# Order of the f32 matmuls in sample attention: strip by strip, or piece by piece over four strips

## Chip, core and metric

The kernel runs on one core of a Trainium2 chip. The metric is the device time of one execution in microseconds; of several runs the median is taken. The engines are named as the profile names them: PE is TensorE (PEld its weight loads), DVE is VectorE, ACT is ScalarE, POOL is GpSimd, and SP issues most of the loads.

## The reference, cut to what matters

The kernel computes one layer of a decoder for 1024 prompt positions and for 8 samples of 4 new positions each, with a cache of 1024 earlier positions for each sample. Only the attention of the samples is touched by the change. Each sample's 4 positions attend, in 12 query heads (3 dilations times 4 key/value heads of 64 dimensions), to 129 positions of cache and new rows that lie 1, 4 or 16 apart:

```
def dilated_attn_sample(q, k_all, v_all, L):
    ...
    for g, (_, dil) in enumerate(DIL_PAIRS):
        idx = L + jnp.arange(T)[:, None] - dil * taps[None, :]
        ...
        s = jnp.einsum('bthd,btkhd->bthk', q[:, :, g], kg, preferred_element_type=jnp.float32) * (HEAD_DIM ** -0.5)
        s = s - (slopes[g] * dil)[:, None] * taps.astype(jnp.float32)[None, :]
        m = jnp.max(s, axis=-1, keepdims=True)
        p = jnp.exp(s - m)
        outs.append(jnp.einsum('bthk,btkhd->bthd', p, vg) / den[..., None])
    return combine_groups(outs, lses)
```

The slope of a head makes far positions count less, and positions before the first are masked. The kernel gets both as a mask that is added to the scores.

## The kernel before, in words

Activations lie with the features on the 128 partitions and the 1056 positions (1024 of the prompt, 32 of the samples) in the columns. Projections multiply in three terms of split halves (`wh`, `wl`), through the helper at L122, in blocks of 352 columns; a block of a projection (`proj`) is 24 matmuls into one of two PSUM banks named `mm`. The weights stream in by SP, are split by ACT (L115) and DVE (L116), and wait in rings of three.

The stage around the change computes the twelve projections of the convolution branch (L1047 on; four features f of three units each). After each block of a projection `tick()` takes one step of a chain of generators: first the mixing of the prompt's attention groups, then four sample groups (`sample_set`, L665 on), then `sample_sum`. After the third feature (f = 2) whatever is left of the chain is written out at once. Which instruction stands where in the queue of an engine is then settled by the framework, which keeps dependences and orders by its own estimate of when inputs are there; in this stage the order of the code isn't pinned.

A sample group is one pair of key/value heads (hp) and four samples (bg): there are four groups. For each, SP loads a mask and five tiles of 1024 columns, `kv[0]` to `kv[4]`, with the cache's keys and values. The four samples of a group are the four strips: sample j has its query weights in 32 columns (`qs`), and its results on the partitions 32 j to 32 j + 31 of a PSUM bank. The steps of a group are these:

- Scores (L682 to L684): for each sample, one matmul over 512 columns of keys into the bank `pa`, one over 128 columns into `pb`, and one over the 32 new positions (`kS`) into `pb`.
- Softmax: DVE adds the mask and takes the maximum (L688, L692), ACT takes the exponential (L698).
- Transposes on PE (L705, L708, L709), copied to `pT` by DVE (L706, L710, L711).
- Values (L719, L723): for each sample five matmuls of 128 keys each against tiles of `kv[2]` to `kv[4]`, and one of the 32 new positions against `v_smp`, all summed in one place of the bank `po`. L719 has 128 rows and 32 columns of weights, L723 32 and 32.
- ACT copies `po` to `oS` (L727).

Between two steps lies a block of a projection, whose bank is emptied by ACT (L1054) or by DVE (L1062). ACT and DVE work through their queues in order, so what stands behind L727 waits for the values too. After the fourth group come `sample_sum` (L812 to L854) and the last three projections.

The prompt's attention, earlier, has a loop of the same kind with two strips of 64 columns (L580): there the head, which selects the strip, is the inner loop.

Of the kernel before, what the change touches and what calls it, by code (L numbers as in the profile page):

```python
# [14 lines left out]
P = 128  # L15
# [3 lines left out]
TS = 32  # L19
# [39 lines left out]
def tile_decoder_step(ctx: ExitStack, tc: tile.TileContext, i, o):  # L59
    nc = tc.nc  # L60
# [16 lines left out]
    def U(dt=F32, w=T):  # L77
        return up.tile([P, w], dt, tag="U", name=nm("U"))
# [8 lines left out]
    def psum(tag=None):  # L87

        if tag is None:
            turn[0] += 1  # L90
            tag = ("mm", "s", "s")[turn[0] % 3]
        return pp.tile([P, 512], F32, tag=tag, name=nm(tag), bufs=banks[tag])
# [4 lines left out]
    def const(name, shape, src=None, dt=F32):  # L97
        t = cp.tile(shape, dt, tag=name, name=name)
        if src is not None:
            fill(t, src)  # L100
        return t

    def small(shape, tag, bufs=2, dt=F32):
        return sp.tile(shape, dt, tag=tag, name=nm(tag), bufs=bufs)
# [33 lines left out]
    def fill(out, in_):  # L138

        with tc.issue_after(pace[0].ins):  # L140
            nc.sync.dma_start(out=out, in_=in_)
# [35 lines left out]
    def rstd(*sums, out=None, soon=True):  # L177

        w = sums[0].shape[-1]
        n = w // 32  # L180
        ps = norm_bank()
        with tc.high_priority() if soon else nullcontext():
            for q, s in enumerate(sums):
                matmul(ps[:, :w], ones, s, start=q == 0, stop=q == len(sums) - 1)

        t = tmp("tb")[:, :w]
        nc.vector.transpose(t, ps[:, :w])
        r = small([P, 12], "r4")[:, :n]
        tv = t.rearrange("p (c q) -> p c q", q=32)
        nc.scalar.activation(r, tv[:, :, 0], AF.Sqrt, bias=eps_t, scale=1.0 / D)  # L190
        nc.vector.reciprocal(r, r)
        nc.vector.tensor_copy(tv, r.unsqueeze(2).to_broadcast([P, n, 32]))
        if out is None:
            out = small([P, LW], "rstd", 1)[:, :w]
        nc.vector.transpose(out, t)
        return out
# [156 lines left out]
    kS = const("kS", [P, 2, TS])  # L353
# [103 lines left out]
    for n in range(9):  # L457
        r = P if n < 8 else TS
# [35 lines left out]
    qs = const("qs", [P, 2, 8, 32])  # L494
# [36 lines left out]
    for g in range(3):  # L531
# [28 lines left out]
        for hp in range(2):  # L560
# [29 lines left out]
            for n in range(8):  # L590
# [8 lines left out]
                for h in range(2):  # L599
# [6 lines left out]
                        start=True,  # L606
                        stop=True,
# [57 lines left out]
    def sample_set(se):  # L665

        hp, bg = se // 2, se % 2
        msk = U()
        fill(msk[:, :NKS], i["maskS"][se])
        kv = [U() for _ in range(5)]  # L670
        for q in range(5):
            fill(kv[q][:, :1024], i["kv"][hp, bg, q])
        if se == 0:
            fill(hmask, i["hmask"])
        for _ in range(3):
            yield
        pa, pb = psum("s"), psum("s")
        for j in range(4):
            b = bg * 4 + j
            qb = qs[:, hp, b, :]  # L680
            r = slice(32 * j, 32 * j + 32)
            nc.tensor.matmul(pa[r, :512], qb, kv[j // 2][:, (j % 2) * 512 : (j % 2 + 1) * 512], start=True, stop=True)  # L682
            nc.tensor.matmul(pb[r, :P], qb, kv[2][:, j * P : (j + 1) * P], start=True, stop=True)
            nc.tensor.matmul(pb[r, P : P + TS], qb, kS[:, hp, :], start=True, stop=True)  # L684
        s = msk
        m0 = small([P, 1], "m0")
        m = stS[:, 0, se : se + 1]
        nc.vector.tensor_tensor_reduce(  # L688
            out=s[:, :512], in0=pa, in1=msk[:, :512], scale=1.0, scalar=-3.0e38,
            op0=ALU.add, op1=ALU.max, accum_out=m0,  # L690
        )
        nc.vector.tensor_tensor_reduce(  # L692
            out=s[:, 512:NKS], in0=pb[:, :160], in1=msk[:, 512:NKS], scale=1.0, scalar=m0,
            op0=ALU.add, op1=ALU.max, accum_out=m,
        )
        nm_ = small([P, 1], "nms")
        nc.vector.tensor_scalar(out=nm_, in0=m, scalar1=-1.0, scalar2=None, op0=ALU.mult)
        nc.scalar.activation(  # L698
            s[:, :NKS], s[:, :NKS], AF.Exp, bias=nm_, accum_out=stS[:, 1, se : se + 1]
        )  # L700
        yield
        pT = U()
        tp = psum("t")
        for c in range(4):
            nc.tensor.transpose(tp[:, c * P : (c + 1) * P], s[:, c * P : (c + 1) * P], ident)  # L705
        nc.vector.tensor_copy(pT[:, :512], tp)  # L706
        tp = psum("t")
        nc.tensor.transpose(tp[:, :P], s[:, 512:640], ident)  # L708
        nc.tensor.transpose(tp[:TS, P : 2 * P], s[:, 640:NKS], ident)  # L709
        nc.vector.tensor_copy(pT[:, 512:640], tp[:, :P])  # L710
        nc.vector.tensor_copy(pT[:TS, 640:768], tp[:TS, P : 2 * P])  # L711
        yield
        po = psum("o")
        for j in range(4):
            r = slice(32 * j, 32 * j + 32)
            for c in range(5):
                m = j * 5 + c + 4
                vc = kv[2 + m // 8][:, (m % 8) * P : (m % 8 + 1) * P]
                nc.tensor.matmul(  # L719
                    po[r, :P], pT[:, c * P + 32 * j : c * P + 32 * j + 32], vc,  # L720
                    start=c == 0, stop=False,
                )
            nc.tensor.matmul(  # L723
                po[r, :P], pT[:TS, 640 + 32 * j : 640 + 32 * j + 32], v_smp[:, hp * P : (hp + 1) * P],
                start=False, stop=True,
            )
        nc.scalar.copy(oS[:, se, :], po[:, :P])  # L727
        yield
# [131 lines left out]
    def conv(f, z, yb):  # L860
# [29 lines left out]
        yield  # L890

    attn = chain(mix_groups(), *(sample_set(se) for se in range(4)), sample_sum())
    taps = iter(())

# [538 lines left out]
    for b, ts in enumerate(LB):  # L1433
        w = ts.stop - ts.start
        before, sums = sums, [small([P, LW], "ssum", 3)[:, :w]]
        for f in range(KD):
# [9 lines left out]
            if f == 1 and b:  # L1446
                r = rstd(*before, soon=False)
# [171 lines left out]
```

## Time and profile before

| what | value |
|---|---|
| median of 3 runs | 1720.37 us (1718.62 to 1722.14) |
| the profiled execution | 1723.34 us, span 1721.6 us |
| mean granted clock of PE | 0.991 |
| PE busy | 1686.6 us, 98% of the span |
| DVE busy | 1018.8 us, 59% |
| ACT busy | 572.9 us, 33% |

The groups of the changed lines, from the view that groups instructions by line: the columns are line, engine, operation, what it writes and reads, count; then the busy time of the group, the mean length of one in ns, and the engine's idle time before them.

```profile
L719 PE MATMUL o<-U,U 128*32 128x128 f32 x160 | 20.5, 275 | 0.0
L682 PE MATMUL s<-U,qs 128*32 128x512 f32 x32 | 13.2, 605 | 0.0
L723 PE MATMUL o<-v_smp,U 32*32 32x128 f32 x32 | 6.4, 280 | 0.0
L683 PE MATMUL s<-U,qs 128*32 128x128 f32 x32 | 5.0, 276 | 0.0
L684 PE MATMUL s<-kS,qs 128*32 128x32 f32 x32 | 3.0, 194 | 0.0
```

Busy time is the time in which at least one instruction of the group runs, so for instructions that overlap it is less than count times length. A matmul's length runs until its last result is out, and the next one can start before that. The forms are the size of the part of PE that is used (rows * columns of weights) and what streams through it (partitions x columns).

### The profile page before, as it was taken

Reading aid. Unit: us, or ns where it says so; the run is one execution under the profiler, and the core shown is the slowest. Engines: PE = TensorE matmul, PEld = TensorE weight load, DVE = VectorE, ACT = ScalarE, POOL = GpSimd, SP = SyncE. Lnnn points to the kernel's source line nnn. Section 1 sums busy time; section 2 is a strip of 40 time slices with the busy share of each in tenths; the row PEclk is TensorE's granted clock in tenths of the full one; section 3 lists DMA queues with packets and bytes.
Section 4 is the critical chain, followed back from the end, with each engine's and each line's share of the span. In section 5 each row is a group of like instructions: output and inputs, shape, how many; then the busy total and the mean of one; then the engine's idle time right before and its main releaser. Section 6 shows DMA issues by size and latency. Waiting matters only on the chain.

```text
span 1721.6 us, 28876 instructions
## 1 busy us (share of the span) xinstructions
PE 1686.6 (98%) x12041; PEld 1624.8 (94%) x12041; DVE 1018.8 (59%) x1895; ACT 572.9 (33%) x1072; POOL 34.4 (2%) x42
## 2 busy tenths in 40 slices
PE   8999999999999999999999899999999999999996
PEld 7999878888889999999999899999999999999996
DVE  7437454453255544557767886555555554777658
ACT  7321243411123333341256563333332224421021
POOL 0001000000000000000000000000000000000005
PEclk9999999999999999999999999999999999999998
DMA  6332212062522232276453403222222224433202
GB/s 214 129 108 101 88 39 62 18 214 77 192 71 98 103 113 101 102 266 205 157 194 129 157 26 100 78 85 83 92 75 75 75 75 175 175 100 116 84 1 101
DMA packets 74410, 191.69 MB, mean 111 GB/s; under 512 B 11836, under 2 KB 33660, under 8 KB 74280
## 3 DMA queue, kind: packets, MB, share of 16 engines
q1 hardware_dynamic: 48624, 144.23, 25.4%
q10 hardware_dynamic: 25656, 45.63, 7.3%
q8 instruction: 94, 1.54, 0.4%
q14 instruction: 36, 0.29, 0.1%
HBM read 143.16 MB, written 46.67 MB: 110 GB/s over the span
## 4 chain that ended last, share of the span: by engine, by line
PE 91%; DVE 5%; issue 1%; ACT 1%; DMA 0%; DVEq 0%; ACTq 0%
PE pair L122 35%; PE mm L122 19%; PE bank L122 14%; PE s L122 12%; PE s L602 2%; PE t L635 1%; PE o L719 1%; PE o L580 1%; PE s L382 1%; PE s L381 1%; PE s L383 1%; DVE U L1426 1%; PE s L682 1%; DVE ssum L1445 1%; DVE wl L116 1%
## 5 line engine op out<-in xcount | busy, mean ns | idle before, releaser
L122 PE MATMUL pair<-U,wh 128*128 128x264 f32 x2880 | 526.5, 284 | 0.0
L122 PEld LDWEIGHTS pair<-U,wh 128*128 128x128 f32 x2880 | 445.9, 188 | 0.0
L122 PE MATMUL pair<-U,wl 128*128 128x264 f32 x1440 | 408.6, 284 | 0.0
L115 ACT CAST wh<-wr 128x512 fp32r<-128x512 f32 (+1 forms) x262 | 191.3, 742 | 512.8 <-PE pair L122 174.6
L122 PE MATMUL mm<-U,wh 128*128 128x352 f32 (+1 forms) x1280 | 316.9, 327 | 2.3 <-ACT U L1054 2.0
L122 PEld LDWEIGHTS pair<-U,wl 128*128 128x128 f32 x1440 | 271.2, 188 | 0.0
L122 PE MATMUL bank<-U,wh 128*128 128x352 f32 (+2 forms) x1056 | 256.0, 325 | 0.2 <-DVE U L116 0.2
L116 DVE TENSOR_TENSOR wl<-wr,wh 128x512 fp32r<-128x512 f32 (+1 forms) x262 | 216.0, 838 | 63.9 <-ACT wh L115 62.2
L122 PEld LDWEIGHTS mm<-U,wh 128*128 128x128 f32 x1280 | 221.4, 190 | 15.1 <-issue 8.8
L122 PE MATMUL mm<-U,wl 128*128 128x352 f32 (+1 forms) x648 | 208.5, 322 | 0.0
L122 PE MATMUL s<-U,wh 128*128 128x352 f32 (+1 forms) x888 | 198.5, 311 | 6.2 <-ACT U L263 5.8
L122 PEld LDWEIGHTS bank<-U,wh 128*128 128x128 f32 x1056 | 185.9, 189 | 1.0 <-DVE U L116 0.5
L122 PE MATMUL bank<-U,wl 128*128 128x352 f32 (+2 forms) x528 | 171.7, 325 | 0.7 <-DVE wl L116 0.7
L122 PEld LDWEIGHTS s<-U,wh 128*128 128x128 f32 x888 | 149.8, 190 | 8.4 <-ACT U L263 6.2
L122 PE MATMUL s<-U,wl 128*128 128x352 f32 (+1 forms) x468 | 144.1, 308 | 0.0
L1413 DVE TENSOR_TENSOR U<-bank,U 128x352 f32<-128x352 f32 x192 | 97.3, 522 | 51.7 <-PE bank L122 51.7
L122 PEld LDWEIGHTS mm<-U,wl 128*128 128x128 f32 x648 | 122.7, 189 | 1.7 <-issue 1.3
L115 ACT CAST U<-U 128x1056 fp32r<-128x1056 f32 (+2 forms) x111 | 82.0, 757 | 91.5 <-DMA U<-a_dram 31.1
L116 DVE TENSOR_TENSOR U<-U,U 128x1056 fp32r<-128x1056 f32 (+2 forms) x111 | 92.6, 856 | 30.8 <-ACT U L115 30.4
L1009 DVE TENSOR_TENSOR tb<-pair,ta 128x528 f32<-128x528 f32 x49 | 34.7, 708 | 120.4 <-PE pair L122 120.4
L122 PEld LDWEIGHTS bank<-U,wl 128*128 128x128 f32 x528 | 99.9, 189 | 1.4 <-DVE wl L116 1.4
L122 PEld LDWEIGHTS s<-U,wl 128*128 128x128 f32 x468 | 88.8, 190 | 0.0
(282 smaller groups left out, 1887.6 us busy)
## 6 DMA issues: line engine op xcount, KB each, us to landing
wr<-in_w SPq DMA_DIRECT2D x143, 512.0 KB, 4.0
sig_dram<-V ACTq DMA_DIRECT2D x24, 528.0 KB, 2.7
V<-sig_dram SPq DMA_DIRECT2D x24, 528.0 KB, 3.7
a_dram<-U ACTq DMA_DIRECT2D x22, 528.0 KB, 5.0
U<-a_dram SPq DMA_DIRECT2D x22, 528.0 KB, 5.2
U<-in_kv SPq DMA_DIRECT2D x20, 512.0 KB, 6.9
U<-outs SPq DMA_DIRECT2D x10, 528.0 KB, 6.5
U<-in_xT SPq DMA_DIRECT2D x24, 176.0 KB, 4.6
```

Of the source, the lines that this page charges most:

```text
L115: nc.scalar.copy(hi, x)
L116: (eng or nc.vector).tensor_tensor(out=lo, in0=x, in1=hi.bitcast(F32), op=ALU.subtract)
L122: ins = nc.tensor.matmul(*a, **k)
L381: nc.tensor.matmul(ps[:, :HV], h_hi[k][:, tk], wv[k][0], start=k == 0, stop=False)
L382: nc.tensor.matmul(ps[:, :HV], h_hi[k][:, tk], wv[k][1], start=False, stop=False)
L383: nc.tensor.matmul(ps[:, :HV], h_lo[k][:, tk], wv[k][0], start=False, stop=k == KD - 1)
L580: nc.tensor.matmul(po[0][h * 64 : (h + 1) * 64, (n % 4) * P : (n % 4 + 1) * P], vg[kb // 4][:, (kb % 4) * 256 + hd : (kb % 4) * 256 + hd + ...
L602: nc.tensor.matmul(ps, qT[hs_, n * P : (n + 1) * P], kg[hp][hs_, k0 : k0 + nk * P], start=True, stop=True,)
L635: last = nc.tensor.transpose(tp[:, at : at + P], pt[:, h, c * P : (c + 1) * P], ident)
L682: nc.tensor.matmul(pa[r, :512], qb, kv[j // 2][:, (j % 2) * 512 : (j % 2 + 1) * 512], start=True, stop=True)
L1009: nc.vector.tensor_tensor(out=out, in0=view(ps), in1=y, op=ALU.add)
L1413: nc.vector.tensor_tensor(out=a, in0=ps, in1=a, op=ALU.add)
```

## The change

Both loops over strips are turned inside out. In the scores, all four samples' matmuls of 512 columns come first, then all four of 128, then all four of 32. In the values the loop over the five pieces of keys is the outer one and the samples are the inner one, and the four matmuls of the new positions stand behind in a loop of their own. Operands, tiles, counts and flags stay the same, and nothing but these PE instructions is moved in the code.

```
         pa, pb = psum("s"), psum("s")
-        for j in range(4):
-            b = bg * 4 + j
-            qb = qs[:, hp, b, :]
-            r = slice(32 * j, 32 * j + 32)
-            nc.tensor.matmul(pa[r, :512], qb, kv[j // 2][:, (j % 2) * 512 : (j % 2 + 1) * 512], start=True, stop=True)
-            nc.tensor.matmul(pb[r, :P], qb, kv[2][:, j * P : (j + 1) * P], start=True, stop=True)
-            nc.tensor.matmul(pb[r, P : P + TS], qb, kS[:, hp, :], start=True, stop=True)
+        rows = [slice(32 * j, 32 * j + 32) for j in range(4)]
+        qb = [qs[:, hp, bg * 4 + j, :] for j in range(4)]
+        for j, r in enumerate(rows):
+            nc.tensor.matmul(
+                pa[r, :512], qb[j], kv[j // 2][:, (j % 2) * 512 : (j % 2 + 1) * 512], start=True, stop=True
+            )
+        for j, r in enumerate(rows):
+            nc.tensor.matmul(pb[r, :P], qb[j], kv[2][:, j * P : (j + 1) * P], start=True, stop=True)
+        for j, r in enumerate(rows):
+            nc.tensor.matmul(pb[r, P : P + TS], qb[j], kS[:, hp, :], start=True, stop=True)
...
         po = psum("o")
-        for j in range(4):
-            r = slice(32 * j, 32 * j + 32)
-            for c in range(5):
+        for c in range(5):
+            for j, r in enumerate(rows):
                 m = j * 5 + c + 4
                 vc = kv[2 + m // 8][:, (m % 8) * P : (m % 8 + 1) * P]
                 nc.tensor.matmul(
                     po[r, :P], pT[:, c * P + 32 * j : c * P + 32 * j + 32], vc,
                     start=c == 0, stop=False,
                 )
+        for j, r in enumerate(rows):
             nc.tensor.matmul(
                 po[r, :P], pT[:TS, 640 + 32 * j : 640 + 32 * j + 32], v_smp[:, hp * P : (hp + 1) * P],
                 start=False, stop=True,
```

## The prediction

> **What bounds the kernel now.** I read the page first (busy shares, then the chain that ended last).
>
> ```profile
> span 1721.6 us, 28876 instructions
> PE 1686.6 (98%) x12041; PEld 1624.8 (94%) x12041; DVE 1018.8 (59%) x1895; ACT 572.9 (33%) x1072; POOL 34.4 (2%) x42
> ...
> PE 91%; DVE 5%; issue 1%; ACT 1%; DMA 0%; DVEq 0%; ACTq 0%
> ```
>
> TensorE is busy for 98% of the span and is 91% of the chain, so time taken out of its stream comes off the end, as long as nothing else becomes late. The changed lines run in the stretch from 376 to 486 us, so I next asked for the busy time by windows, there and behind it.
>
> ```profile
> 376.00:486.00 110.00, 107.98 (x705) 90.43 (x704) 31.19 (x80) 14.85 (x29) 0.00 (x0) 0.99 0.41 149
> 486.00:530.00 44.00, 44.00 (x263) 43.65 (x263) 31.82 (x39) 16.18 (x21) 0.00 (x0) 0.95 0.27 87
> 530.00:600.00 70.00, 70.00 (x560) 70.00 (x560) 33.06 (x51) 25.03 (x42) 0.00 (x0) 1.00 0.23 88
> ```
>
> The columns are the length, the busy time of TensorE, its weight loads, VectorE, ScalarE and GpSimd, the clock, the DMA share and GB/s. TensorE is busy for 107.98 of the 110 us; VectorE has 31.19 us of work and ScalarE 14.85. Behind it TensorE has no idle time up to 600. So this stage ends when TensorE's stream ends, and the stages behind take over any shift.
>
> Then I asked for windows cut to the changed stages themselves, each from the first matmul of a stage to the start of the next matmul that isn't of it. The last row of each answer adds the stages up: first the scores of groups 1 to 3 (L682 to L684), then the values of all four groups (L719, L723).
>
> ```profile
> sum 11.76, PE 11.76 PEld 5.68 DVE 1.04 ACT 0.90 POOL 0.00; mean PE 3.92 PEld 1.89 DVE 0.35 ACT 0.30 POOL 0.00
> ```
> ```profile
> sum 24.64, PE 24.64 PEld 18.29 DVE 7.13 ACT 0.45 POOL 0.00; mean PE 6.16 PEld 4.57 DVE 1.78 ACT 0.11 POOL 0.00
> ```
>
> Three score stages of 3.92 us and four value stages of 6.16, all of it TensorE alone. The scores of group 4 look different, and they are used below.
>
> **What a strip costs now.** The timeline of the first score stage shows what one strip waits for (start, length, what). Every f32 matmul call is two instructions, which I call passes; the rows count them (x2 for the first strip's one call of L682).
>
> ```profile
> 379.76 1.05 PE L682 MATMUL s<-U,qs 128*32 128x512 f32 x2
> ...
> 380.65 0.62 PE L682 MATMUL s<-U,qs 128*32 128x512 f32 x1
> 380.75 0.27 PE L683 MATMUL s<-U,qs 128*32 128x128 f32 x1
> ...
> 380.86 0.23 PE L684 MATMUL s<-kS,qs 128*32 128x32 f32 x2
> 381.10 0.59 PE L682 MATMUL s<-U,qs 128*32 128x512 f32 x1
> ...
> 381.53 0.27 PE L683 MATMUL s<-U,qs 128*32 128x128 f32 x1
> ```
>
> Inside a strip a pass starts when the one before has been streamed: 381.53 - 381.10 = 0.43 us for 512 columns (0.45 for the first pass of a run, 381.10 - 380.65), 380.86 - 380.75 = 0.11 for 128. For the 32 columns of L684 I estimate a quarter of that, 0.03. The next strip's first pass begins at 380.65, while the first strip still has a pass of L683 (380.75) and both of L684 (380.86) to start. So two strips do run beside each other, and a later matmul in another strip starts ahead of earlier ones. Still, the wide passes of the four strips come one after another: the second strip's start 380.65 - 379.76 = 0.89 us behind the first's.
>
> The values show no overlap at all. Rows of TensorE's own timeline, from a narrow window last:
>
> ```profile
> 392.37 1.28 PE L719 MATMUL o<-U,U 128*32 128x128 f32 x10
> 393.58 0.40 PE L723 MATMUL o<-v_smp,U 32*32 32x128 f32 x2
> 393.91 1.28 PE L719 MATMUL o<-U,U 128*32 128x128 f32 x10
> ```
> ```profile
> 398.00 0.27 PE L719 MATMUL o<-U,U 128*32 128x128 f32 x1
> 398.20 0.40 PE L723 MATMUL o<-v_smp,U 32*32 32x128 f32 x2
> 398.53 0.43 PE L122 MATMUL mm<-U,wh 128*128 128x352 f32 x1
> ```
>
> Each strip is ten passes of tile 128*32, then two of tile 32*32, and the next strip starts only after them: 393.91 - 392.37 = 1.54 us, four times. The step from one tile size to the other takes 398.20 - 398.00 = 0.20 us where a pass of the same tile would follow after 0.11, and the way back out of L723 takes 398.53 - 398.20 = 0.33 for its two passes and the switch.
>
> **What four strips cost side by side.** Group 4 shows it already. Its scores were split up by the framework that orders the instructions: two strips of L682, then projection matmuls, the other two strips, more projection, and all of L683 and L684 together.
>
> ```profile
> 466.28 1.05 PE L682 MATMUL s<-U,qs 128*32 128x512 f32 x4
> 467.26 0.43 PE L122 MATMUL mm<-U,wh 128*128 128x352 f32 x1
> ...
> 470.90 0.45 PE L683 MATMUL s<-U,qs 128*32 128x128 f32 x8
> 471.14 0.26 PE L684 MATMUL s<-kS,qs 128*32 128x32 f32 x8
> 471.34 0.43 PE L122 MATMUL mm<-U,wh 128*128 128x352 f32 x1
> ```
>
> Four passes of 512 columns in two strips take 1.05 us, which is what the two of one strip took at 379.76: the second strip is free. Eight passes of 128 columns in four strips take 0.45 us, where two in one strip take 0.40 (L723 rows): all four run together, and the fourth lags by about 0.04 us. The prompt's attention says the same of two strips for longer, twelve passes of L580 (64 columns each) in 0.88 us, where ten in one strip take 1.28:
>
> ```profile
> 200.87 0.88 PE L580 MATMUL o<-tb,U 128*64 128x128 f32 x12
> ```
>
> **The change, part by part.** It removes and adds no instruction; it puts the four strips of one piece next to each other.
>
> Scores of groups 1 to 3. In each strip the six passes follow one another as now: 0.45 + 0.43 for L682, 0.11 + 0.11 for L683, 0.03 for L684; add 0.04 of lag and 0.13 for the way back to the projection's tile (471.34 less the last start of L684, which I put at 471.14 + 0.03 + 0.04 = 471.21). That is 1.30 us instead of 3.92: 2.62 less, three times, 7.9 us.
>
> Scores of group 4. They stay as they are if the framework splits them as before, so 0. If it doesn't, the three pieces (467.26 - 466.28 = 0.98 twice, 471.34 - 470.90 = 0.44) become one of 1.30, and two entries of about 0.09 go: another 1.3 us. Split like this, groups 1 to 3 would lose the same 1.3 us each, 3.9. I take neither: these bounds go to the range.
>
> Values, four groups. Ten passes of a strip have their starts spread over 1.28 - 0.27 = 1.01 us; with lag 1.05 for four strips at once. Then one switch, 0.20, and L723 with its way out, 0.33 + 0.04. That is 1.62 us instead of 6.16: 4.54 less, four times, 18.2 us. About 0.55 of each 4.54 is the six switches that go (0.09 each); the rest is overlap.
>
> Waits. The fourth strip's first value matmul needs the last of the five loaded tiles, which is asked for now only in the third strip; the matmuls of the next projection are queued behind such a wait. What it costs is bounded by when the tiles land.
>
> ```profile
> L141 SPq DMA_DIRECT2D U<-in_kv x20: 327/404/646, 348.8 to 446.3; - x20
> ...
> DMA to landing us min/median/max: 3.6/6.9/9.4
> ```
>
> The last load is issued at 446.3 and lands by 446.3 + 9.4 = 455.7. The scores of group 4 start at 466.28. Between the issue and the scores lie the shortened scores and values of group 3, 2.6 + 4.5 = 7.1 us, so the scores come 466.28 - 446.3 - 7.1 = 12.9 us behind the last issue, over 9.4; the values come later still. Earlier groups have longer. So I take nothing. The softmax between scores and values (VectorE, ScalarE) is covered by a block of 24 projection matmuls as now, at 0.16 us each (below) 3.9 us. If a wait comes after all, its price is itself and perhaps a clock drop:
>
> ```profile
> 481.54 0.27 ACT L727 COPY V<-o 128x128 f32<-128x128 f32 x1 [8.47 <-PE o L723]
> ...
> 483.84 0.95 PE L122 MATMUL mm<-U,wh 128*128 128x352 f32 x2 [2.02 <-ACT U L1054]
> ```
> ```profile
> 483.80:491.00 7.20, 7.16 (x26) 6.76 (x27) 5.73 (x15) 0.38 (x2) 0.00 (x0) 0.54 0.27 97
> 491.00:530.00 39.00, 39.00 (x244) 38.85 (x244) 27.35 (x32) 16.12 (x21) 0.00 (x0) 1.00 0.30 99
> ```
>
> Behind the last values ScalarE had stood at L727; the copies that empty the projection's banks were queued behind it, and TensorE idled 2.0 us. Then the clock was 0.54 for 7.2 us: 26 matmuls, which at the next row's 39.00/244 = 0.16 us each would take 4.2, so 3.0 us were lost. The order behind the last values is unchanged, so I leave both in; the drop may go (3.0 less) or come once more (3.0 more). The Trainium skill ("TensorE: Matmul & The Clock Gate", Part 1) says that the clock halves after an idle window of about 3.4 us; this trace shows a drop after 2.0 us, so the row sets my bound. By the skill's length neither 3.0 would belong to the range.
>
> Sum: 7.9 + 18.2 = 26.1 us. The profiled execution took 1723.34 us, its span of 1721.6 and 1.7 around it; so 1697.2 for it. It stands 2.97 above the median of the three runs, 1720.37, so I forecast a median of **1694.3 us**.
>
> **Rivals.**
> *Overlap, but only in part.* Either no more than two strips stream at once, or matmuls start strictly in program order, so that a strip's second pass holds up the next strip and each new strip costs one pitch. Two at once: values 1.62 + 1.01 = 2.63 and scores 1.30 + 0.88 + 0.25 = 2.43, a gain of 4 x 3.53 + 3 x 1.5 = 18.6, 1701.8 us. In order: values 20 x 0.11 (a second pass with the next strip's first) + 0.9 for L723 and its switches = 3.1, scores 4 x (0.43 + 0.11 + 0.03) + 0.15 = 2.4, a gain of 4 x 3.06 + 3 x 1.5 = 16.7, 1703.7. For it: 512 columns in four strips, and more than 0.45 us of four strips, are in no row. Against it: the start at 380.65 ahead of 380.75, and the eight passes in 0.45. The second form is what the Trainium skill would have ("TensorE: Matmul & The Clock Gate", Part 3, The mechanism): it says that matmuls start and end strictly in program order; the rows at 380.65 and 470.90 differ from that.
> *TensorE idles behind each shortened stage* (the slower side). ScalarE stands at the copy behind a stage until the stage ends, as at 481.54, and the two banks of the projection aren't emptied in time; each place pays 2.3 us of idle (483.84 - 481.54) and 3.0 of low clock, 5.3. Six shortened stages have no such gap now (groups 1 to 3): 6 x 5.3 = 31.8 - 26.1 = 5.7 us slower, 1726. It decides from five stages on (26.5). For it: the rows at 481.54. Against: at 398.53 the projection follows the values at once, and a shorter stage holds ScalarE for less time.
> *The change doesn't take effect.* The framework orders instructions by its own idea of when inputs arrive, as in group 4, and puts the strips one by one again: 1720. Against: in groups 1 to 3 the trace follows the order of the code.
>
> **How the numbers follow.** The forecast gets 0.90, partial overlap 0.06, idling 0.02, no effect 0.02. Its own range: 1694.3 - 1.3 - 3.0 = 1690.0 to 1694.3 + 3.9 + 3.0 = 1701.2; the runs shown lie up to 1.8 from their median (1718.62 to 1722.14), so 1688 to 1703, which also takes in the first form of partial overlap. About 0.2% (3.4 us) is what a measurement can tell from no change. Faster: 0.90 + 0.06 = 0.96; same 0.02; slower 0.02.
>
> **What would show it.** In the new timeline: L719 as one row of 40 passes of some 1.3 us, followed by one row of eight passes of L723; L682 as eight passes in about 1.1 us; the next projection 1.6 and 1.3 us behind the first matmul. Value stages over 2.5 us mean partial overlap; a projection that names ScalarE or VectorE as what it waited for, with a clock near 0.5 behind it, means idling. Wrong outright: stages as short as said but an end that hasn't moved, with TensorE's idle time grown elsewhere.

## The result, and the profile after

| what | before | after |
|---|---|---|
| median | 1720.02 us (4 runs, 1718.62 to 1722.14) | 1693.64 us (4 runs, 1691.83 to 1695.26) |
| profiled execution, span | 1723.34 us, 1721.6 us | 1693.98 us, 1692.2 us |

The ratio is 0.9846 (95% interval 0.9834 to 0.9858): 26.4 us less in the medians, where 26.1 was forecast. The page of the changed kernel, with the busy shares and the chain that ended last:

```profile
span 1692.2 us, 28872 instructions
PE 1657.3 (98%) x12041; PEld 1604.4 (95%) x12041; DVE 1018.9 (60%) x1895; ACT 573.1 (34%) x1072; POOL 34.5 (2%) x42
...
PE 92%; DVE 4%; issue 1%; ACT 1%; DMA 0%; DVEq 0%; ACTq 0%
```

As many matmuls as before, but TensorE is busy for 29.3 us less (1686.6 to 1657.3), and its share of the span is the same 98%. VectorE and ScalarE do the same work in the shorter span.

The first group in TensorE's timeline after the change; L681, L685 and L687 are the scores (L682 to L684 before), L721 and L726 the values (L719 and L723 before):

```profile
379.08 1.06 PE L681 MATMUL s<-U,qs 128*32 128x512 f32 x8
379.97 0.40 PE L685 MATMUL s<-U,qs 128*32 128x128 f32 x8
380.19 0.24 PE L687 MATMUL s<-kS,qs 128*32 128x32 f32 x8
380.36 0.43 PE L122 MATMUL mm<-U,wh 128*128 128x352 f32 x1
```
```profile
389.03 1.30 PE L721 MATMUL o<-U,U 128*32 128x128 f32 x40
390.26 0.42 PE L726 MATMUL o<-v_smp,U 32*32 32x128 f32 x8
390.61 0.59 PE L122 MATMUL mm<-U,wh 128*128 128x352 f32 x2
```

The counts are what to look at. Forty passes of L721 lie in one row of 1.30 us; before, ten took 1.28. Eight passes of 512 columns take 1.06 us, where the two of a single strip took 1.05. The windows over the stages, cut as before (sum rows; three score stages, four value stages):

```profile
sum 3.82, PE 3.82 PEld 1.90 DVE 0.89 ACT 0.90 POOL 0.00; mean PE 1.27 PEld 0.63 DVE 0.30 ACT 0.30 POOL 0.00
```
```profile
sum 6.32, PE 6.32 PEld 4.73 DVE 2.58 ACT 0.45 POOL 0.00; mean PE 1.58 PEld 1.18 DVE 0.65 ACT 0.11 POOL 0.00
```

11.76 - 3.82 = 7.94 us for the scores (7.9 forecast) and 24.64 - 6.32 = 18.32 for the values (18.2 forecast): 26.26 in all. The scores of group 4 are split into three pieces as before. Behind the last values TensorE idles as before, for the same time:

```profile
456.87 0.59 PE L122 MATMUL mm<-U,wh 128*128 128x352 f32 x2 [2.02 <-ACT U L1057]
```

The two profiled executions differ by more than the stages, 29.4 us of span. One part of the rest is the clock behind that idle time:

```profile
456.80:464.00 7.20, 7.13 (x35) 6.58 (x36) 6.53 (x16) 0.84 (x5) 0.00 (x0) 0.76 0.42 138
```

Before, the same 7.2 us had a clock of 0.54 and 26 matmuls; here it is 0.76 and 35. Nine matmuls of 0.16 us are 1.4 us. Of the remaining 1.7 us, 0.7 lie ahead of the first changed stage (it starts at 379.76 before and at 379.08 after) and most of the rest near 980 us of the kernel before, where the clock is 0.50 for 6.8 us (from 978.5); in the changed kernel the same place (from 952.8) has it at 0.50 for 3.4 us. The profiled execution of before was itself 3.3 us over its median. So the 26.4 of the medians is the number to compare with.

### The profile page after: what moved, and what is told of

It reads as the page before. It is cut to its first block, busy times and chain, and to the rows that moved or that the text cites. A ratio compares the mean times of both kernels' runs of the same rounds, so it can differ in the third digit from the quotient of the medians.

```text
span 1692.2 us, 28872 instructions
## 1 busy us (share of the span) xinstructions
PE 1657.3 (98%) x12041; PEld 1604.4 (95%) x12041; DVE 1018.9 (60%) x1895; ACT 573.1 (34%) x1072; POOL 34.5 (2%) x42
## 4 chain that ended last, share of the span: by engine, by line
PE 92%; DVE 4%; issue 1%; ACT 1%; DMA 0%; DVEq 0%; ACTq 0%
PE pair L122 36%; PE mm L122 19%; PE bank L122 14%; PE s L122 12%; PE s L602 2%; PE t L635 1%; PE o L580 1%; PE s L381 1%; PE s L382 1%; PE s L383 1%; DVE U L1429 1%; DVE ssum L1448 1%; PE mm L381 0%; PE mm L383 0%; PE mm L382 0%
```

## The experiments

The theory is the forecast's: passes of different strips stream beside each other, all four of them, and what the stages lose on TensorE comes off the end. The rivals: the switches of tile size were what the values lost; matmuls start strictly in program order; the gain needs both halves or comes from what lies behind. How far ahead a strip can be filled doesn't follow from the two kernels alone, so that was measured too.

**values_only and scores_only.** Each half of the change alone.

```
values_only: scores as before
-        for j, r in enumerate(rows): (three loops, L680 to L687)
+        for j in range(4): (one loop with L683 to L685)
scores_only: values as before
-        for c in range(5):
-            for j, r in enumerate(rows):
+        for j in range(4):
+            r = slice(32 * j, 32 * j + 32)
+            for c in range(5):
                 ...
-        for j, r in enumerate(rows): (the loop of the new positions, which go back into the loop over j)
```

> Only the values are turned piece by piece; the scores stay strip by strip. If the gains are what the stages lose on TensorE and nothing else moves: value stages 1.58 us (before 6.16), score stages 3.92 in groups 1 to 3, 4 x 4.58 = 18.3 us under the kernel before, about 1701.7. If part of the gain came from the two halves together (the framework's order, the clock behind the last values), it differs from that by more than 2 us.

> Only the scores are turned; the values stay strip by strip. Adding up: score stages 1.28 us in groups 1 to 3, values 6.16, 3 x 2.64 = 7.9 us under the kernel before, about 1712.1. If the halves don't add up: more than 2 us off that.

values_only ran in 1702.63 us, 0.990 of the kernel before (0.9885 to 0.9915): 17.2 less than its 1719.85. scores_only ran in 1710.93, 0.9947 (0.9932 to 0.9962): 8.9 less. The windows of the first group, scores and then values, of values_only:

```profile
379.03:382.95 3.92, 3.92 (x25) 1.89 (x24) 0.17 (x1) 0.45 (x1) 0.00 (x0) 1.00 1.04 415
391.63:393.21 1.58, 1.58 (x49) 1.18 (x49) 0.52 (x1) 0.00 (x0) 0.00 (x0) 1.00 0.46 189
```

and of scores_only:

```profile
379.20:380.48 1.28, 1.28 (x26) 0.64 (x25) 0.14 (x1) 0.45 (x1) 0.00 (x0) 1.00 1.01 390
389.16:395.32 6.16, 6.16 (x50) 4.57 (x49) 0.52 (x1) 0.00 (x0) 0.00 (x0) 1.00 0.10 39
```

Each half has exactly the stage of its own kind, and the two gains add up to 26.1, near the 26.4 of the whole. That one is 1.1 below and the other 1.0 above the sum of its stages is within the 2 us that were allowed. The profiles offer a reason: the 7.2 us behind the last values, with the same 2.0 us of idle ahead of them, in values_only and then in scores_only:

```profile
464.78:471.98 7.20, 7.18 (x36) 6.67 (x37) 6.61 (x16) 0.84 (x4) 0.00 (x0) 0.76 0.40 133
```
```profile
475.30:482.50 7.20, 7.08 (x44) 6.65 (x45) 6.65 (x16) 2.13 (x6) 0.00 (x0) 1.00 0.31 104
```

scores_only has no low clock there, 44 matmuls instead of 36. That is 8 x 0.16 = 1.3 us. Of the runs that weren't profiled, only the mean granted clock is on record, and it points the same way as the profiles: 0.993 in all four runs of values_only, 0.994 to 0.996 in those of scores_only, 0.993 to 0.995 in the seven of the kernel before beside them. Where the clock fell in those runs isn't recorded, so this is a reason that fits and isn't shown.

**ten_passes, four_passes, six_passes.** These keep the scores of the change and give the values in longer turns of a strip, with the matmuls of the new positions behind.

```
ten_passes
-        for c in range(5):
-            for j, r in enumerate(rows):
+        for j, r in enumerate(rows):
+            for c in range(5):
four_passes, six_passes
-        for c in range(5):
-            for j, r in enumerate(rows):
+        for turn in ((0, 1), (2, 3), (4,)):      (six_passes: ((0, 1, 2), (3, 4)))
+            for j, r in enumerate(rows):
+                for c in turn:
                     ...
```

> As the changed kernel, but the values go strip by strip (ten passes each), with the matmuls of the new positions in their own loop behind. So the switches of tile size are gone and the order of the pieces is the old one. Theory 1, a strip takes four passes ahead (one that streams, three that wait) and the fifth holds up all that is behind it: the next strip starts with the seventh pass, 0.68 us behind the one before, and the stage is 3 x 0.68 + 1.01 + 0.6 = 3.6 us. Theory 2, strict program order of starts: the next strip starts with the tenth pass, 1.01 behind, stage 4.6 us. Theory 3, the switches were what the values lost: the stage is close to 1.6 us in this order too.

> As the changed kernel, but a strip's turn is two pieces of keys (four passes), then the next strip. If a strip takes four passes ahead, nothing is held up and the value stage is 1.6 us as in the changed kernel. If it took only three, every turn would hold the next strip up by a pass of 0.11 to 0.14, and the stage would be over 2.2 us.

> As the changed kernel, but a strip's turn is three pieces (six passes), then two. With four taken ahead, strip j + 1 starts with the third pass of strip j, 0.24 us behind it, the fourth at 0.74, and the second turn no longer holds up anything: last start 0.74 + 1.01 = 1.75, stage 2.3 us. With eight or more taken ahead it would be 1.6 us, with starts strictly in program order over 3 us.

The first value stage of each, from the first value matmul to the next projection matmul: ten_passes, six_passes, four_passes.

```profile
389.50 3.33 PE L721 MATMUL o<-U,U 128*32 128x128 f32 x40
392.76 0.42 PE L726 MATMUL o<-v_smp,U 32*32 32x128 f32 x8
393.12 0.43 PE L122 MATMUL mm<-U,wh 128*128 128x352 f32 x1
```
```profile
389.09 2.02 PE L722 MATMUL o<-U,U 128*32 128x128 f32 x40
391.04 0.42 PE L727 MATMUL o<-v_smp,U 32*32 32x128 f32 x8
391.39 0.43 PE L122 MATMUL mm<-U,wh 128*128 128x352 f32 x1
```
```profile
388.54 1.34 PE L722 MATMUL o<-U,U 128*32 128x128 f32 x40
389.81 0.42 PE L727 MATMUL o<-v_smp,U 32*32 32x128 f32 x8
390.16 0.43 PE L122 MATMUL mm<-U,wh 128*128 128x352 f32 x1
```

The stages are 393.12 - 389.50 = 3.62, 391.39 - 389.09 = 2.30 and 390.16 - 388.54 = 1.62 us: 3.6, 2.3 and 1.6 were worked out from one number, four passes taken ahead for a strip. Strict program order (4.6, over 3) and switches alone (1.6 for ten_passes) are excluded. ten_passes also splits the values' gain: without the switches between strips, and with the overlap that four passes ahead allow in the old order, the stage goes from 6.16 to 3.62; the order of the change brings the other 2.04. The times: ten_passes 1701.96 us (2 runs; 0.9896 of the kernel before, 0.9877 to 0.9916), that is 8.3 over the changed kernel, 4 x 2.04 = 8.2 by the stages. four_passes gave 1695.59 in its one run; its stages ask for 0.2 more than the change, and the rest of the 2.0 is within the scatter of single runs (the changed kernel's four reach 1695.26). six_passes gave 1694.25 in its one run, where its stages ask for 4 x 0.72 = 2.9 more than the change. Its profile shows that the stages did cost that: the last value stage starts at 455.10 us, where it is 452.89 in the changed kernel, 2.2 later for the three stages before it. Behind it six_passes has the full clock in three places where the changed kernel's profile has 0.50 for 3.4 us (behind the last values, from 894.8 and from 952.8), which gives the time back. Behind the last values:

```profile
459.80:467.00 7.20, 7.09 (x44) 6.64 (x45) 6.65 (x16) 2.15 (x6) 0.00 (x0) 1.00 0.30 101
```

**switches.** Piece by piece as in the change, but each of the four matmuls of tile 32*32 stands behind a piece of its own.

```
         for c in range(5):
             for j, r in enumerate(rows):
                 ...
-                    start=c == 0, stop=False,
+                    start=c == 0, stop=c == 4,
                 ...
-        for j, r in enumerate(rows):
-            nc.tensor.matmul(po[r, :P], pT[:TS, 640 + 32 * j : ...], v_smp[...], start=False, stop=True)
+            if c < 4:
+                r = rows[c]
+                nc.tensor.matmul(po[r, :P], pT[:TS, 640 + 32 * c : ...], v_smp[...], start=False, stop=False)
```

> As the changed kernel, but the four matmuls of the new positions (tile 32*32) are put behind the first four pieces, one behind each, so that PE changes the tile size eight times inside the stage instead of once. If each change makes all strips run empty first: a piece takes 0.15 + 0.20 + 0.33 = 0.69 us, the stage 4 x 0.69 + 0.35 = 3.1 us. If changes are cheap beside strips that run: 1.6 to 1.8 us.

The first two pieces and the last in TensorE's timeline:

```profile
389.03 0.43 PE L721 MATMUL o<-U,U 128*32 128x128 f32 x8
389.39 0.40 PE L727 MATMUL o<-v_smp,U 32*32 32x128 f32 x2
389.72 0.42 PE L721 MATMUL o<-U,U 128*32 128x128 f32 x8
...
391.78 0.43 PE L721 MATMUL o<-U,U 128*32 128x128 f32 x8
392.13 0.43 PE L122 MATMUL mm<-U,wh 128*128 128x352 f32 x1
```

A piece with its switches takes 389.72 - 389.03 = 0.69 us and the stage 3.10, as worked out. A change of tile size lets all strips run empty, so what stands between two changes can't overlap with what lies beyond them. In group 3 the framework split this stage in two, in group 4 it took 3.39 us; the other stages are 3.10. In all that is 6.4 us more than in the changed kernel; the one run took 1700.81 us, 7.2 more.

**spread and spread_on.** The change left 2.0 us of idle, a low clock and the split scores of group 4 where they were. All three stand where the chain's remains are written out at once. spread goes on with a step a block through the last feature; spread_on goes on through the first two gate units too.

```
spread
         if f == 2:
-            left(attn)
             others = halves(0, *quarters(0))
+    left(attn)
     left(others)
spread_on: not here, but in the first two gate units
             next(others, None)
+            next(attn, None)
         nc.scalar.dma_start(out=sig_dram[u], in_=sig)
     left(others)
+    left(attn)
```

> As the changed kernel, but what is left of the sample groups behind the third feature isn't written out at once; it goes on one step a block through the last feature. If the split scores of group 4, the idle 2.0 us behind the last values and the low clock after it come from writing it all at once: scores of group 4 in one stage of 1.28 us, no idle over 1 us behind the last values, the clock stays at 1.0, and the time is 4 to 6 us under the changed kernel, 1687.5 to 1689.5. If the chain of the last sums only moves behind, into the first gates: no gain, 1693 to 1696, or slower if the loads of the halves come late.

> As spread, but the steps that are still left behind the last feature go on, one a block, through the first two gate units, instead of being written out at once there. In spread the idle time came back at 480 to 490 us, where TensorE stood at a transpose of the last sums (4.4 us) with no projection left to run. If that was all that cost spread its gain: scores of group 4 in one stage of 1.28 us, no idle over 1 us from 440 to 500, clock 1.0 there, 4 to 6 us under the changed kernel, 1687.5 to 1690. If the chain delays something behind (the gates' loads, the attention outputs): 1692 or more.

spread missed: 1697.27 us, 3.6 more than the change. The scores of group 4 did come together and the gap behind the last values went, but a longer one begins 26 us later than that one did in the changed kernel (480.93 against 454.84), in its timeline:

```profile
480.60 0.33 PE L122 MATMUL mm<-U,wl 128*128 128x352 f32 x1
485.01 0.19 PE L843 MATMUL t<-ident,ta 4*128 4x4 f32 x1 [4.08 <-DVE ta L840]
```

TensorE stands at a transpose of the last sums, which waits for a chain on VectorE and ScalarE; no projection is left ahead of it in the queue, and the first gate unit is queued behind. That is the second of the two outcomes on record, but over its 1693 to 1696: a gap of this size (4.4 us between starts) wasn't in it. Behind the gap the clock is 0.50 for 6.8 us (485.5 to 492.3). spread_on, which gives this chain more blocks to hide behind, ran in 1689.66 us, 0.9824 of the kernel before (0.9811 to 0.9837), inside the time that was expected, with one gap of 1.2 us between starts (0.88 of it idle), over the 1 us on record:

```profile
460.77 1.07 PE L681 MATMUL s<-U,qs 128*32 128x512 f32 x8
...
488.35 0.32 PE L122 MATMUL s<-U,wl 128*128 128x352 f32 x1
489.54 0.66 PE L854 MATMUL t<-selS,V 128*128 128x16 f32 x4 [0.88 <-DVE V L851]
```
```profile
444.00:476.00 32.00, 32.00 (x285) 29.99 (x275) 20.35 (x27) 9.72 (x16) 0.00 (x0) 1.00 0.42 134
476.00:500.00 24.00, 23.06 (x145) 22.39 (x144) 21.21 (x45) 10.89 (x16) 0.00 (x0) 1.00 0.28 94
```

The scores of group 4 are one stage, TensorE has no idle time from 444 to 476, and the clock is 1.00 in both windows.

**after_again and spread_on_again.** Both once more on one chip, for a direct comparison.

> The changed kernel once more, beside the next one on the same chip: 1693 to 1695 us, 26.4 under the kernel before, within 1.5.

> The same kernel as spread_on. If its gain over the changed kernel is the idle time and low clock behind the last values (2.3 us of idle and about 1.7 of clock in the changed kernel's profile) and the three pieces of group 4's scores (1.3 us), less the 1.2 us it idles at 488 us: about 4 us under the changed kernel of this call, 1689 to 1691. If it was the chip: no difference over 1 us.

1693.76 us (0.9842 of the kernel before, 0.9828 to 0.9855) and 1689.65 us (0.9822, 0.9808 to 0.9835): 4.1 us between them, and 4.0 between the medians of the first two. The sum worked out for it is 2.3 of idle, 1.4 of clock and 1.3 for the scores, less 1.2 for the gap at 488: 3.8. The version that goes on step by step is the fastest of this case.

## Why the prediction was right, by its steps

- *TensorE's stream sets the end there.* Right. What the stages lost, 26.26 us, is the loss of the median, 26.4, within the scatter of the runs; each half alone shows its own part.
- *Scores of groups 1 to 3, 1.30 us each.* Measured 1.27 to 1.28 (3.82 in three). The lag of 0.04 for the fourth strip and the rounding up were too much here by 0.02 to 0.03.
- *Scores of group 4 stay split.* They did. Had they come together, another 1.3 us would have been gained by the prediction's estimate; spread_on shows them together, in 1.27 us.
- *Values, 1.62 us each.* Measured 1.58; the lag, counted twice, is as large as the difference. The part ascribed to switches, 0.55 of 4.54, was worked out for switches alone. ten_passes puts 2.54 us on the new positions' own loop in the old order, 6.16 to 3.62: with the switches gone, strips could overlap as far as four passes ahead allow, which the sum hadn't named as a part. It changes no forecast, since the change has both.
- *The loads come in time.* They do: the last is issued at 430.9 and takes at most 9.5 us.

```profile
L141 SPq DMA_DIRECT2D U<-in_kv x20: 327/388/539, 348.2 to 430.9; - x20
...
DMA to landing us min/median/max: 3.4/6.7/9.5
```

  That is 440.4 by then; the scores of group 4 start at 443.91, 13.0 behind the issue, where 12.9 was worked out. (The block that covers the softmax is 24 x 0.16 = 3.84 us, not 3.9; nothing hangs on it.)
- *The idle time and the low clock behind the last values may stay, go or come again.* The idle time is the same 2.0 us in both kernels, the clock dropped less. The range's 3.0 us was the right size for what the clock can do: 44, 35 or 26 matmuls in the 7.2 us behind the same gap. The reason given for the idle time was misread, though. ScalarE's copy at L727 was over at 481.54 + 0.27 = 481.81, just when TensorE's idle time began. What ScalarE stood at then was the next instruction in its queue, the exponential of `sample_sum`, which waits for a chain on VectorE; only behind it come the copies that empty the projection's banks. In the kernel before:

```profile
483.14 0.31 ACT L827 ACTIVATE ta<-ta 4x128 f32<-4x128 f32 x1 [1.34 <-DVE ta L826]
483.36 0.77 ACT L1054 COPY U<-mm 128x352 f32<-128x352 f32 x2
```

  This chain comes once, behind the last values, whatever the length of the stages, so the same 2.02 us stand in the changed kernel too (there L830, at 456.17).
- *Rivals.* Partial overlap, in both forms, falls with the x40 and x8 rows, and strict order again with six_passes and ten_passes. The Trainium skill's rule that matmuls start strictly in program order ("TensorE: Matmul & The Clock Gate", Part 3, The mechanism) doesn't hold for these passes. By that order the stage of ten_passes would take 4.6 us, and it takes 3.62. Idling behind each stage didn't occur: behind the values of groups 1 to 3 TensorE goes on at once. The rival had its reason from the misread row; the copy of `po` holds up nothing that can be seen here, and it was the chain of the last sums that made TensorE idle, 2.0 us before and after, and with a wait at one of its transposes 4.1 us in spread.

## What to carry to other kernels

Where TensorE sets the end and several f32 matmuls use separate strips of the array, put them next to each other in the order of the instructions, and group those of another tile size in a block of their own. Read from the trace how many passes of one strip go ahead before they hold up the next: here turns of up to four passes cost next to nothing (1.58 and 1.62 us), six cost 0.7 and ten 2.0. Then look at what stands behind the shortened stages: here a chain of small steps on VectorE and ScalarE, written out at once, was worth another 4 us when it was spread over more blocks (spread_on), and cost 3.6 us when it was spread over too few (spread). When an engine waits, read what stands at the head of its queue at that moment.

## What the runs showed of the hardware that was not expected

- A strip takes four f32 passes ahead, one that streams and three that wait; the fifth holds up every later matmul, of other strips too. One number gives the stages of 3.62, 2.30 and 1.62 us, and the 0.89 us from strip to strip before the change (two wide passes, until the four narrow ones are all in). This was measured for f32 passes of tile 128*32 alone.
- Behind the same gap of 2.0 us without matmuls the clock of the next 7.2 us was 0.54 in the kernel before, 0.76 in the changed one and in values_only, and 1.00 in scores_only: 26, 35 and 36, and 44 matmuls. In narrower windows the clock is either 0.50 or 1.00, and the low stretch is 6.8 us long before (two of 3.4) and 3.4 us after:

```profile
483.57:486.98 3.41, 3.14 (x10) 2.75 (x11) 1.94 (x11) 0.56 (x2) 0.00 (x0) 0.50 0.64 228
486.99:490.39 3.40, 3.40 (x14) 3.40 (x13) 3.37 (x7) 0.00 (x0) 0.00 (x0) 0.50 0.00 0
490.41:494.00 3.59, 3.59 (x24) 3.44 (x24) 2.25 (x3) 2.08 (x5) 0.00 (x0) 1.00 0.06 9
```
```profile
457.90:461.31 3.41, 3.41 (x13) 3.00 (x12) 2.94 (x10) 0.00 (x0) 0.00 (x0) 0.50 0.51 169
461.32:464.70 3.38, 3.38 (x24) 3.23 (x24) 3.35 (x3) 1.16 (x4) 0.00 (x0) 1.00 0.03 5
```

  Before, it begins 0.3 us ahead of TensorE's next matmul (483.57 against 483.84); in the changed kernel 1.0 us behind it (457.90 against 456.87). How long the gap is doesn't settle whether none, one or two such stretches follow; what does isn't shown here.
- Four strips of f32 with 512 columns each stream at the pace of one (1.06 us for eight passes, 1.05 for two), so neither reading four streams nor writing one bank in four places cost time that can be seen.
